# Where the rows of the stationary operand begin: a decoder block with the pads of its activation tiles taken out

## The chip, the cores and the metric

The kernel runs on one core of a Trainium2 chip. The metric is the time of one execution on the device in microseconds (us). A profile of one further execution says, engine by engine, what ran when: TensorE (PE, with its weight loads listed apart as PEld), VectorE (DVE), ScalarE (ACT), GpSimd (POOL) and SyncE (SP, which issues the transfers). A line number such as L305 is a line of the kernel's file.

## The reference

The kernel computes one decoder block for 256 tokens of width 2048, in float32:

```
mod = silu(c) @ w_ada + b_ada                      # six rows: shift, scale, gate, twice
hn  = rmsnorm(x, norm1_g) * (1 + sc1) + sh1
proj = hn @ w_in                                   # 2048 x 10256: q k v, z, beta, a, glu, two gates
o   = chunk_gated_delta_rule(...)  ;  branch_a = (norm(o) * silu(z)) @ dn_w_o
u   = causal_dwconv(val * sigmoid(gl), 31 taps) ;  branch_b = silu(layernorm(u)) @ cf_w_o
x   = x + gt1 * ((sigmoid(ga) * branch_a + sigmoid(gb) * branch_b) @ w_out)
hn  = rmsnorm(x, norm2_g) * (1 + sc2) + sh2
gate, up = split(hn @ w_up)                        # 2048 x 11264
x   = x + gt2 * ((silu(causal_dwconv(gate, 3 taps)) * up) @ w_down)      # 5632 x 2048
out = rmsnorm(x, final_norm_g)
```

## The kernel before

Nearly all of the work is products of the activations (256 tokens) with large weight matrices. `product` (L283) does each of them for 512 columns of weights at a time. It walks over the rows of the weights in chunks of two row tiles (2 x 128 rows x 512 columns). A chunk `w` is loaded by a transfer, ScalarE casts it to the rounded type fp32r (`wh`, L293), VectorE takes the difference (`wl`, L295), and TensorE then does 12 matmuls: for each row tile `kk` of the chunk and each half `t` of the tokens one of high activations with `wh` (L305), one of low activations with `wh` (L306) and one of high activations with `wl` (L307). So two rounded parts stand for each float32 number. `w`, `wh` and `wl` are rings of 5, 3 and 3 buffers in the pool `p0`.

In these matmuls the activations are the stationary operand: 128 rows (features) by 128 columns (tokens) are loaded into the array, and 512 columns of weights stream through as the moving operand. So each matmul has a weight load, and in the trace the load for the next matmul lies beside the matmul before it.

The stationary operands are tiles with a high and a low part. `hn` holds both for all 16 row tiles, of 256 tokens each, in one tile; `mg` (the merged mixers, for `w_out`) and `hn2` (for the feed-forward part) use the same place later (tag "hn", L345, L826, L871). In the program before, this tile has a pad of one number behind each row tile: `[P, 2, KD, S + 1]`, of which 0 to S are used. The products over it are called p1, qkv, glu, gb, z, ga (all over `w_in`), out, up1, gate and up. Some of them go over the row tiles in parts (0 to 3, 4 to 9, 10 to 15, `R3`), as the modulation gets ready; others over all 16 at once.

The other stationary operands are `cfh` and `cfl` (L813, L814; product cfo with `cf_w_o`), `oh0`, `ol0`, `oh1`, `ol1` (L794 to L798; product dno with `dn_w_o`) and `h` (L933; product down with `w_down`). `h` is made for each group `g` of 512 columns of the feed-forward part, in a high and a low tile of 4 row tiles each; the last product goes over groups 0 to 5 in a first half and 6 to 10 in a second, with tiles h0 to h5 used again. ScalarE writes the high parts by a cast (L936 for `h`, L263 for `hn`), VectorE the low parts by a difference (L937, L264).

The order of the instructions on each engine is set when the program is built, by a scheduler that follows priorities (the `Band` objects) and its own estimate of times. The places of the tiles in the on-chip memory follow from the pools: each tag has a place of the size of its largest tile, in the order in which the tags first appear. So `hn`'s size decides where the rings `w`, `wh` and `wl` behind it begin.

In the program before, `hn` begins at byte 40160 of each partition, the buffers of `wh` at 97632, 101728 and 105824, those of `wl` at 109920, 114016 and 118112. All of these are 96 past a multiple of 128. The tiles `h`, `oh`, `ol`, `cfh` and `cfl` all begin 64 past a multiple of 128.

Of the kernel before, what the change touches and what calls it, by code (L numbers as in the profile page):

```python
# [9 lines left out]
F32R = mybir.dt.float32r  # L10
# [4 lines left out]
P = 128  # L15
D = 2048
S = 256
KD = D // P
# [4 lines left out]
FF = 5632  # L23
FT = FF // P
EPS = 1e-6
C_Z, C_B, C_GLU, C_GA, C_GB = 3072, 4096, 4112, 6160, 8208

VEC = {}
# [27 lines left out]
def block_kernel(ctx: ExitStack, tc, x, vec, ab, rowv, w_ada, w_in, dn_w_o, cf_w_o, w_out, w_up, w_down, out):  # L56
# [6 lines left out]
    p0 = ctx.enter_context(tc.tile_pool(name="p0", bufs=1))  # L63
# [43 lines left out]
    eps = p0.tile([P, 1], F32, name="eps")  # L107
    nc.gpsimd.memset(eps, EPS)
    mone = p0.tile([P, 16], F32, name="mone")
# [115 lines left out]
    def rstd_col(ss):  # L225

        a = p0.tile([P, 2], F32, tag="nrm_a", name="nrm_a")
        nc.vector.tensor_reduce(out=a, in_=ss, axis=mybir.AxisListType.X, op=ALU.add)
        nc.gpsimd.tensor_scalar(out=a, in0=a, scalar1=1.0 / D, scalar2=EPS, op0=ALU.mult, op1=ALU.add)
        r = p0.tile([P, 2], F32, tag="nrm_c", bufs=3, name="nrm_c")  # L230
# [3 lines left out]
    def rstd_of(pt, pool=pd, tag="dl"):  # L234

        a = p0.tile([P, 2], F32, tag="nrm_a", name="nrm_a")
        nc.vector.tensor_scalar(out=a, in0=pt[:, 0:2], scalar1=EPS, scalar2=None, op0=ALU.add)
        return spread(a, pool, tag)
# [80 lines left out]
    p1 = mix.enter_context(tc.tile_pool(name="p1", bufs=1))  # L319
    su = tc.tile_pool(name="su", bufs=1)  # L320
    sup = su.__enter__()
    with b_first():
        x_sb = p0.tile([P, KD, S], F32, tag="x", name="x_sb")
        xv = x.rearrange("(t p) n -> p t n", p=P)
        xt = p1.tile([P, 2, D], F32, tag="HS", name="xt")
        for q in range(2):
            for t in range(2):
                nc.sync.dma_start(out=xt[:, t, q * 1024:(q + 1) * 1024], in_=xv[:, t, q * 1024:(q + 1) * 1024])
        nc.sync.dma_start(out=vt, in_=vec)
        ss1 = p0.tile([P, 2, 2], F32, name="ss1")  # L330
        for q in range(2):
            for t in range(2):
                sq = p1.tile([P, 1024], F32, tag=("QA", "KA")[t], name="sq")
                nc.scalar.activation(out=sq, in_=xt[:, t, q * 1024:(q + 1) * 1024], func=AF.Square, accum_out=ss1[:, t, q:q + 1])
        r1 = rstd_col(ss1)
        for q in range(4):
            qs = slice(q * 512, (q + 1) * 512)
            for t in range(2):
                nc.vector.tensor_scalar(out=xt[:, t, qs], in0=xt[:, t, qs], scalar1=r1[:, t:t + 1], scalar2=None, op0=ALU.mult)
            for i in range(2):  # L340
                k = 4 * q + 2 * i
                nc.scalar.copy(out=x_sb[:, k:k + 2, :], in_=turned(xt, (k, k + 1), pd, f"dl{i}"))
        for j in (1, 0):
            drain(ada_block(j, 0, sup, 6, shared=True))
        hn = p0.tile([P, 2, KD, S + 1], F32R, tag="hn", name="hn")[:, :, :, 0:S]  # L345
        modulate(0)
    hh, hl = (lambda k: hn[:, 0, k, :]), (lambda k: hn[:, 1, k, :])

# [14 lines left out]
    def into(parts, add):  # L363

        def evac(pts):
            for d, pt in zip(parts, pts):
                if add:
                    with b_first():
                        nc.vector.tensor_tensor(out=d, in0=pt, in1=d, op=ALU.add)
                else:  # L370
                    nc.scalar.copy(out=d, in_=pt)
        return evac

    def both(t, g=0):
        return [t[:, i, 512 * g:512 * (g + 1)] for i in range(2)]
# [415 lines left out]
        product("z", rows(w_in, C_Z + 512 * g), whole, hh, hl, evac)  # L791
        zs.append(z)
    with b_delta():
        oh0 = p1.tile([P, 4, S], F32R, tag="VA", name="oh0")  # L794
        ol0 = p1.tile([P, 4, S], F32R, tag="QB", name="ol0")
        delta_out(0, on0, zs[0], oh0, ol0)
        oh1 = p1.tile([P, 4, S], F32R, tag="QA", name="oh1")
        ol1 = p1.tile([P, 4, S], F32R, tag="KA", name="ol1")  # L798
        delta_out(1, on1, zs[1], oh1, ol1)

    half8 = (0, 8)
# [8 lines left out]
    with b_delta():  # L810
        cfs = []
        for g in range(4):
            hi = p1.tile([P, 2, S], F32R, tag=f"u{g}", name="cfh")  # L813
            lo = p1.tile([P, 2, S], F32R, tag=f"gl1{g}", name="cfl")  # L814
            nc.scalar.copy(out=hi, in_=cfa[g])
            nc.vector.tensor_tensor(out=lo, in0=cfa[g], in1=hi.bitcast(F32), op=ALU.subtract)
            cfs.append((hi, lo))
# [5 lines left out]


    side_rate[0] = 0.7
    mg = p0.tile([P, 2, KD, S + 1], F32R, tag="hn", name="mg")[:, :, :, 0:S]  # L826
    for g in range(4):
        def evac(pts, g=g):
            for pt, a, b in zip(pts, both(ga, g), both(gb, g)):
# [36 lines left out]
    p2 = ctx.enter_context(tc.tile_pool(name="p2", bufs=1))  # L866
    spare.append(True)
    gt_home[5] = lambda piece: p2.tile([P, 512], F32, tag=f"gt{piece}", name="gt2")
    with b_first():
        r2 = rstd_col(ss2)  # L870
    hn2 = p0.tile([P, 2, KD, S + 1], F32R, tag="hn", name="hn2")[:, :, :, 0:S]  # L871

    def modulate2(part):
        k0, k1 = R3[part]
# [23 lines left out]
    for half, (g0, g1) in enumerate(((0, 6), (6, 11))):  # L898
        nt = 4 * (g1 - g0)
        hf = {}  # L900
        for g in range(g0, g1):
            sg = p2.tile([P, 4, S], F32, tag="fsg", bufs=2, name="fsg")
            ks = last if g < NG else whole
            side_rate[0] = 0 if g < NG else 0.4

            def whole_sums(pts, g, i):
                if g < NG:
                    into(both(pre[2 * g + i]), True)(pts)
                    return pre[2 * g + i]
                t = p2.tile([P, 2, 512], F32, tag=f"h5{i}", name="sums")  # L910
                into(both(t), False)(pts)
                return t

            def evac_gate(pts, g=g, sg=sg):
                src = whole_sums(pts, g, 0)
                for h in range(2):
                    bank = turned(src, (2 * h, 2 * h + 1))
                    for u in range(2):
                        j = 2 * h + u
                        n = (4 * g + j) * 3  # L920
                        nc.scalar.activation(out=sg[:, j, :], in_=bank[:, u, :], func=AF.Copy, scale=V("ffconv", n + 2))
                        for sft in (1, 2):
                            nc.vector.scalar_tensor_tensor(
                                out=sg[:, j, sft:], in0=bank[:, u, 0:S - sft], scalar=V("ffconv", n + 2 - sft), in1=sg[:, j, sft:], op0=ALU.mult, op1=ALU.add)
                nc.scalar.activation(out=sg, in_=sg, func=AF.Silu)

            def evac_up(pts, g=g, sg=sg):
                src = whole_sums(pts, g, 1)
                for h in range(2):
                    bank = turned(src, (2 * h, 2 * h + 1), pd, f"dl{h}")  # L930
                    s2 = sg[:, 2 * h:2 * h + 2, :]
                    nc.vector.tensor_tensor(out=s2, in0=bank, in1=s2, op=ALU.mult)
                hf[g - g0] = [p2.tile([P, 4, S], F32R, tag=f"h{g - g0}{i}", name=f"h{g}{i}") for i in range(2)]  # L933
                for i in range(2):
                    sl = slice(2 * i, 2 * i + 2)
                    nc.scalar.copy(out=hf[g - g0][0][:, sl, :], in_=sg[:, sl, :])  # L936
                    nc.vector.tensor_tensor(out=hf[g - g0][1][:, sl, :], in0=sg[:, sl, :], in1=hf[g - g0][0][:, sl, :].bitcast(F32), op=ALU.subtract)  # L937

            product("gate", rows(w_up, 512 * g), ks, gh, gl, evac_gate)
            product("up", rows(w_up, FF + 512 * g), ks, gh, gl, evac_up)  # L940
        if half == 0:
            raw = p2.tile([P, 2, D], F32, tag="raw", name="raw")
            for g in range(4):
                product("down", rows(w_down, 512 * g, 4 * g0), (0, nt), lambda k: hf[k // 4][0][:, k % 4, :], lambda k: hf[k // 4][1][:, k % 4, :], into(both(raw, g), False))
            continue
        need((5, 0), (5, 1))
        fg_row = p2.tile([P, D], F32, name="fg_row")
        nc.sync.dma_start(out=fg_row, in_=rowv[:, 2 * D:].to_broadcast([P, D]))
        with b_ada():
            for g in range(4):  # L950
                for d, r in zip(both(raw, g), both(res, g)):
                    nc.vector.tensor_tensor(out=d, in0=d, in1=gt_row(5, g), op=ALU.mult)
                    nc.vector.tensor_tensor(out=r, in0=d, in1=r, op=ALU.add)
        for g in range(4):
            def evac(pts, g=g):
                add_to_res(5, g, ss3)(pts)
                with b_first():
                    for r in both(res, g):
                        nc.vector.tensor_tensor(out=r, in0=r, in1=fg_row[:, 512 * g:512 * (g + 1)], op=ALU.mult)
            product("down", rows(w_down, 512 * g, 4 * g0), (0, nt), lambda k: hf[k // 4][0][:, k % 4, :], lambda k: hf[k // 4][1][:, k % 4, :], evac)  # L960
# [53 lines left out]
```

## Time and profile before

| what | value |
|---|---|
| time, median of 3 runs (lowest, highest) | 1603.07 us (1601.51, 1603.42) |
| the profiled execution: its time, its span | 1604.07 us, 1602.4 us |
| TensorE busy | 1547.4 us, 97% of the span |
| VectorE, ScalarE busy | 1189.7 us (74%), 809.8 us (51%) |
| mean share of the TensorE clock granted | 0.991 |
| transfers | 366.59 MB, 229 GB/s |

Busy time is the time in which at least one instruction of the engine ran. Matmuls overlap in the pipeline, so the time of one matmul (some 0.4 us in the lists) is longer than the distance from its start to the next one's start; that distance is what the engine's time is made of.

### The profile page before, as it was taken

To read this page: it belongs to the slowest core of one execution; us is meant where nothing else is said; L and a number is where in the kernel's file an instruction comes from. 1 tells how busy PE (TensorE), PEld (TensorE's weight loads), DVE (VectorE), ACT (ScalarE), POOL (GpSimd) and SP (SyncE) were. 2 spreads that over 40 slices of the span, in tenths; PEclk is the share of its full clock that TensorE was granted. 3 is DMA by queue.
4 is the path that set the end of the run, shared out by engine and by line. 5 is a ranking of instruction groups with operands and counts; after the bars stand their busy time and mean duration, and the time that the engine had idled before them with its cause. 6 is when DMAs were issued, how large, how long until landed. Compare 5 with 4: busy or idle time off the path is not lost.

```text
span 1602.4 us, 20092 instructions
## 1 busy us (share of the span) xinstructions
PE 1547.4 (97%) x7198; PEld 1256.9 (78%) x7198; DVE 1189.7 (74%) x1556; ACT 809.8 (51%) x1221; POOL 56.5 (4%) x116
## 2 busy tenths in 40 slices
PE   5999999999999999999979999999999999999996
PEld 5787887788888878787758877888888788788885
DVE  5889967689998967896778789887445587755554
ACT  3554434777687555544346434555444444454442
POOL 2000000400002000000000000000000000000000
PEclk9999999999999989999989999999999999999998
DMA  9999865534467728789778899655556677555552
GB/s 335 385 346 342 267 193 176 158 113 131 148 215 228 245 92 275 259 264 320 260 261 303 299 320 305 204 162 179 185 185 228 224 256 268 191 177 186 183 189 94
DMA packets 182860, 366.59 MB, mean 229 GB/s; under 512 B 12516, under 2 KB 30948, under 8 KB 182632
## 3 DMA queue, kind: packets, MB, share of 16 engines
q1 hardware_dynamic: 182760, 365.31, 68.5%
q8 instruction: 56, 0.92, 0.2%
q14 instruction: 44, 0.36, 0.1%
HBM read 363.17 MB, written 2.10 MB: 228 GB/s over the span
## 4 chain that ended last, share of the span: by engine, by line
PE 85%; DMA 5%; DVE 5%; issue 1%; ACT 1%; POOL 1%; SPq 0%; POOLq 0%; ACTq 0%; DVEq 0%
PE mm_up L307 6%; PE mm_up L305 6%; PE mm_up L306 6%; PE mm_down L306 5%; PE mm_down L305 5%; PE mm_down L307 5%; DMA ada_w<-in_w_ada 4%; PE mm_p L307 4%; PE mm_p L305 4%; PE mm_p L306 4%; PE mm_gate L307 3%; PE mm_gate L306 3%; PE mm_gate L305 3%; PE turned L86 2%; PE mm_ga L307 2%; DVE ada_acc L166 2%
## 5 line engine op out<-in xcount | busy, mean ns | idle before, releaser
L293 ACT CAST wh<-w 128x1024 fp32r<-128x1024 f32 x488 | 512.2, 1051 | 573.9 <-PE mm_up L306 132.9
L295 DVE TENSOR_TENSOR wl<-w,wh 128x1024 fp32r<-128x1024 f32 x488 | 594.2, 1222 | 254.7 <-ACT wh L293 251.8
L166 DVE SCALAR_TENSOR_TENSOR ada_acc<-ada_w,c_act,ada_acc 128x768 f32<-128x768 f32 (+2 forms) x236 | 243.0, 1030 | 84.5 <-DMA ada_w<-in_w_ada 81.3
L305 PE MATMUL mm_up<-wh,hn 128*128 128x512 f32 x472 | 187.8, 400 | 0.4 <-ACT hn L263 0.4
L306 PE MATMUL mm_up<-wh,hn 128*128 128x512 f32 x472 | 187.6, 397 | 0.0
L307 PE MATMUL mm_up<-wl,hn 128*128 128x512 f32 x472 | 174.9, 399 | 0.4 <-DVE wl L295 0.4
L305 PE MATMUL mm_down<-wh,h 128*128 128x512 f32 x352 | 139.8, 397 | 0.0
L306 PE MATMUL mm_down<-wh,h 128*128 128x512 f32 x352 | 139.5, 396 | 0.0
L307 PE MATMUL mm_down<-wl,h 128*128 128x512 f32 x352 | 126.3, 397 | 0.0
L305 PE MATMUL mm_p<-wh,hn 128*128 128x512 f32 x280 | 111.7, 402 | 2.1 <-ACT hn L263 2.0
L306 PE MATMUL mm_p<-wh,hn 128*128 128x512 f32 x280 | 111.1, 399 | 0.0
L305 PEld LDWEIGHTS mm_up<-wh,hn 128*128 128x128 f32 x472 | 89.2, 189 | 21.5 <-ACT hn L263 0.8
L307 PEld LDWEIGHTS mm_up<-wl,hn 128*128 128x128 f32 x472 | 88.7, 188 | 22.1 <-DVE wl L295 1.6
L306 PEld LDWEIGHTS mm_up<-wh,hn 128*128 128x128 f32 x472 | 88.8, 188 | 20.9 <-issue 0.5
L307 PE MATMUL mm_p<-wl,hn 128*128 128x512 f32 x280 | 100.8, 401 | 0.6 <-DVE wl L295 0.5
L305 PE MATMUL mm_gate<-wh,hn 128*128 128x512 f32 x232 | 92.2, 397 | 0.0
L306 PE MATMUL mm_gate<-wh,hn 128*128 128x512 f32 x232 | 91.7, 395 | 0.0
L307 PE MATMUL mm_gate<-wl,hn 128*128 128x512 f32 x232 | 86.0, 397 | 0.0
L307 PEld LDWEIGHTS mm_down<-wl,h 128*128 128x128 f32 x352 | 66.3, 188 | 16.1
L306 PEld LDWEIGHTS mm_down<-wh,h 128*128 128x128 f32 x352 | 66.3, 188 | 16.0
L305 PEld LDWEIGHTS mm_down<-wh,h 128*128 128x128 f32 x352 | 66.3, 188 | 16.0
L428 DVE SCALAR_TENSOR_TENSOR cfa<-u,vt,cfa 128x256 f32<-128x256 f32 x176 | 76.2, 481 | 0.3
(309 smaller groups left out, 2491.8 us busy)
## 6 DMA issues: line engine op xcount, KB each, us to landing
w<-in_w_up SPq DMA_DIRECT2D x176, 512.0 KB, 4.6
w<-in_w_in SPq DMA_DIRECT2D x130, 512.0 KB, 4.3
ada_w<-in_w_ada SPq DMA_DIRECT2D x96, 512.0 KB, 5.0
ada_w<-in_w_ada SPq DMA_DIRECT2D x128, 384.0 KB, 5.3
w<-in_w_down SPq DMA_DIRECT2D x88, 512.0 KB, 3.6
w<-in_w_in SPq DMA_DIRECT2D x64, 256.0 KB, 3.7
w<-in_w_out SPq DMA_DIRECT2D x32, 512.0 KB, 5.7
w<-in_cf_w_o SPq DMA_DIRECT2D x16, 512.0 KB, 4.3
```

What stands on the lines that cost most here:

```text
L86: nc.tensor.transpose(out=out, in_=in_, identity=ident[0:n, 0:n])
L166: nc.vector.scalar_tensor_tensor(out=acc[:, 0:n], in0=wt[:, i, :], scalar=c_act[:, k:k + 1], in1=acc[:, 0:n], op0=ALU.mult, op1=ALU.add)
L293: nc.scalar.copy(out=wh, in_=w)
L295: nc.vector.tensor_tensor(out=wl, in0=w, in1=wh.bitcast(F32), op=ALU.subtract)
L305: nc.tensor.matmul(pts[t], lhsT=xh(k)[:, ts], rhs=wh[:, kk, :], start=(k == k0), stop=False)
L306: nc.tensor.matmul(pts[t], lhsT=xl(k)[:, ts], rhs=wh[:, kk, :], start=False, stop=False)
L307: nc.tensor.matmul(pts[t], lhsT=xh(k)[:, ts], rhs=wl[:, kk, :], start=False, stop=(k == k1 - 1))
L428: nc.vector.scalar_tensor_tensor(out=acc[:, i, :], in0=us[g][:, i, k:k + S], scalar=V("cfconv", (2 * g + i) * CFK + k), in1=acc[:, i, :], ...
```

## The change

Three kinds of edit, all of them on where a tile's rows begin.

First, `hn`, `mg` and `hn2` lose the pad: the row tiles are 256 numbers apart instead of 257. The tile gets 128 bytes smaller, and everything behind it in the pool moves by 128 bytes; `wh` and `wl` then begin at 97504 and 109792 (again 96 past a multiple of 128).

Second, a helper `at` makes a tile that is `room` numbers larger than it needs to be and returns the part that begins `first` numbers into it.

Third, `h`, `oh`, `ol`, `cfh` and `cfl` are made by it. The table `H_AT` has the starts of h0 to h5, `CF_AT` those of `cfh`, `O_AT` those of `oh0`, `ol0`, `oh1`, `ol1`.

```
+H_AT, CF_AT, O_AT = (9, 10, 11, 12, 14, 4), (0, 16, 32, 48), (0, 8, 8, 0)
...
-        hn = p0.tile([P, 2, KD, S + 1], F32R, tag="hn", name="hn")[:, :, :, 0:S]
+        hn = p0.tile([P, 2, KD, S], F32R, tag="hn", name="hn")
...
+    def at(pool, n, first, room, tag, name):
+
+        t = pool.tile([P, n * S + room], F32R, tag=tag, name=name)
+        return t[:, first:first + n * S].rearrange("p (n s) -> p n s", n=n)
...
-        oh0 = p1.tile([P, 4, S], F32R, tag="VA", name="oh0")
-        ol0 = p1.tile([P, 4, S], F32R, tag="QB", name="ol0")
+        oh0 = at(p1, 4, O_AT[0], 8, "VA", "oh0")
+        ol0 = at(p1, 4, O_AT[1], 8, "QB", "ol0")
...
-        oh1 = p1.tile([P, 4, S], F32R, tag="QA", name="oh1")
-        ol1 = p1.tile([P, 4, S], F32R, tag="KA", name="ol1")
+        oh1 = at(p1, 4, O_AT[2], 8, "QA", "oh1")
+        ol1 = at(p1, 4, O_AT[3], 8, "KA", "ol1")
...
-            hi = p1.tile([P, 2, S], F32R, tag=f"u{g}", name="cfh")
-            lo = p1.tile([P, 2, S], F32R, tag=f"gl1{g}", name="cfl")
+            hi = at(p1, 2, CF_AT[g], 48, f"u{g}", "cfh")
+            lo = at(p1, 2, 0, 0, f"gl1{g}", "cfl")
...
-    mg = p0.tile([P, 2, KD, S + 1], F32R, tag="hn", name="mg")[:, :, :, 0:S]
+    mg = p0.tile([P, 2, KD, S], F32R, tag="hn", name="mg")
...
-    hn2 = p0.tile([P, 2, KD, S + 1], F32R, tag="hn", name="hn2")[:, :, :, 0:S]
+    hn2 = p0.tile([P, 2, KD, S], F32R, tag="hn", name="hn2")
...
-                hf[g - g0] = [p2.tile([P, 4, S], F32R, tag=f"h{g - g0}{i}", name=f"h{g}{i}") for i in range(2)]
+                hf[g - g0] = [at(p2, 4, H_AT[g - g0], 16, f"h{g - g0}{i}", f"h{g}{i}") for i in range(2)]
```

The two built programs have the same instructions in the same order on every engine. What differs is addresses. Take the distance of an operand to be where it begins, less where the moving operand in `wh` or `wl` begins, as a remainder of 128 bytes:

| stationary operand | distance before | distance after |
|---|---|---|
| hn, mg, hn2, row tile k, high | 4k (0 to 60) | 0 |
| the same, low | 64 + 4k (64 to 124) | 0 |
| h0 to h5, high | 96 | 4, 8, 12, 16, 24, 112 |
| h0 to h5, low | 96 | 68, 72, 76, 80, 88, 48 |
| cfh of groups 0 to 3; cfl | 96; 96 | 64, 0, 64, 0; 64 |
| oh0 and ol0; oh1 and ol1 | 96; 96 | 64; 0 |

## Rows read from the trace of the kernel before

**Rows 1.** The page: its head, the engines' busy time, the chain by engine.
```profile
span 1602.4 us, 20092 instructions
...
PE 1547.4 (97%) x7198; PEld 1256.9 (78%) x7198; DVE 1189.7 (74%) x1556; ACT 809.8 (51%) x1221; POOL 56.5 (4%) x116
...
PE 85%; DMA 5%; DVE 5%; issue 1%; ACT 1%; POOL 1%; SPq 0%; POOLq 0%; ACTq 0%; DVEq 0%
```

**Rows 2.** Groups: engine, out<-in, count | busy us, mean ns | idle before.
```profile
L293 ACT CAST wh<-w 128x1024 fp32r<-128x1024 f32 x488 | 512.2, 1051 | 573.9 <-PE mm_up L306 132.9 <-PE mm_down L306 130.8 <-PE mm_p L306 63.4
...
L305 PE MATMUL mm_down<-wh,h 128*128 128x512 f32 x352 | 139.8, 397 | 0.0
...
L305 PE MATMUL mm_dno<-wh,oh 128*128 128x512 f32 x64 | 25.6, 402 | 0.0
...
L305 PE MATMUL mm_cfo<-wh,cfh 128*128 128x512 f32 x64 | 25.2, 401 | 0.9 <-ACT cfh L815 0.9
```

**Rows 3.** Timeline, one product: start us, duration us; row tiles 0 to 9, 12, end.
```profile
1240.17 0.40 PE L305 MATMUL mm_gate<-wh,hn 128*128 128x512 f32 x1
...
1241.58 0.40 PE L305 MATMUL mm_gate<-wh,hn 128*128 128x512 f32 x1
...
1242.98 0.40 PE L305 MATMUL mm_gate<-wh,hn 128*128 128x512 f32 x1
...
1244.38 0.40 PE L305 MATMUL mm_gate<-wh,hn 128*128 128x512 f32 x1
...
1245.76 0.39 PE L305 MATMUL mm_gate<-wh,hn 128*128 128x512 f32 x1
...
1247.15 0.40 PE L305 MATMUL mm_gate<-wh,hn 128*128 128x512 f32 x1
...
1248.55 0.39 PE L305 MATMUL mm_gate<-wh,hn 128*128 128x512 f32 x1
...
1249.94 0.39 PE L305 MATMUL mm_gate<-wh,hn 128*128 128x512 f32 x1
...
1251.40 0.39 PE L305 MATMUL mm_gate<-wh,hn 128*128 128x512 f32 x1
...
1252.80 0.39 PE L305 MATMUL mm_gate<-wh,hn 128*128 128x512 f32 x1
...
1256.97 0.39 PE L305 MATMUL mm_gate<-wh,hn 128*128 128x512 f32 x1
...
1258.35 0.40 PE L305 MATMUL mm_gate<-wh,hn 128*128 128x512 f32 x1
...
1262.53 0.39 PE L305 MATMUL mm_up<-wh,hn 128*128 128x512 f32 x1
```

**Rows 4.** Timeline of TensorE in the first mm_down: two starts, 14 steps apart.
```profile
1187.23 0.39 PE L305 MATMUL mm_down<-wh,h 128*128 128x512 f32 x1
...
1190.51 0.39 PE L307 MATMUL mm_down<-wl,h 128*128 128x512 f32 x1
```

**Rows 5.** Timeline of TensorE, three passes of row 0: first, cheapest, last.
```profile
60.55 0.40 PE L305 MATMUL mm_p<-wh,hn 128*128 128x512 f32 x1
...
61.95 0.40 PE L305 MATMUL mm_p<-wh,hn 128*128 128x512 f32 x1
...
1287.46 0.39 PE L305 MATMUL mm_gate<-wh,hn 128*128 128x512 f32 x1
...
1288.83 0.39 PE L305 MATMUL mm_gate<-wh,hn 128*128 128x512 f32 x1
...
1451.70 0.39 PE L305 MATMUL mm_up<-wh,hn 128*128 128x512 f32 x1
...
1453.09 0.40 PE L305 MATMUL mm_up<-wh,hn 128*128 128x512 f32 x1
```

**Rows 6.** ScalarE's casts by tile: count, ns least/median/most, first and last start.
```profile
L263 ACT CAST hn<-t x32: 390/407/429, 40.5 to 976.9; 128x256 fp32r<-128x256 f32 x32
...
L936 ACT CAST h<-fsg x22: 612/621/625, 1020.6 to 1482.6; 128x512 fp32r<-128x512 f32 x22
```

## The prediction

> **What bounds the kernel now.** I read the page first. The span is 1602.4 us, TensorE is busy for 1547.4 us of it (97%), and the chain of waits runs through TensorE for 85% of the span [rows 1]. So time is won or lost where TensorE spends its steps, not in a wait. Next, the groups of instructions: 488 casts of a chunk of weights [rows 2], each of which feeds 12 matmuls of 128x512, make 5856 of them. mm_down is 3 x 352 = 1056, mm_dno and mm_cfo are 3 x 64 each, 384 together [rows 2]; that leaves 4416 for the products whose stationary operand is a row of hn or mg. TensorE stands idle for 0.0 us before the matmuls of mm_down and mm_dno shown and 0.9 us before those of mm_cfo [rows 2], so inside these products next to nothing is waited for.
>
> Then the timeline of one product that nothing interrupts, 96 matmuls from 1240.17 to 1262.53 us [rows 3]. What counts is the step, the time from one matmul's start to the next one's: 22.36 us / 96 = 232.9 ns. The duration beside each (0.39, 0.40) overlaps the next and is not the step. The loading of the stationary operands, 1256.9 us for 7198 of them [rows 1] or 175 ns each, lies beside the matmuls. Each row k of hn serves six matmuls in a row (three for each half of the tokens), and the starts listed are those of a row's first matmul. Row 7 needs 1.46 us for its six, 243.3 ns a step; row 12 needs 1.38 us, 230.0 ns; the others lie between, from 1.38 to 1.41 us (a listed start is good to 0.01 us, 1.7 ns a step). The work of a row is the same for every row; what differs is where it starts. In the program before, rows are 257 numbers apart, and the rings wh and wl begin at 96 bytes past a multiple of 128, so the high part of row k begins 4k bytes past the rings' remainder (of 128 bytes), and its low part 4k + 64. In mm_down every operand, high and low, stands at 96. There 14 steps take 1190.51 - 1187.23 = 3.28 us [rows 4], 234.3 ns each. So the step depends on the distance by a few ns, and a few ns on 5856 steps are what this change is about: 1 ns on all is 5.9 us, 0.37%.
>
> **The change, part by part.** No instruction is added, taken away or moved: the order on every engine is the same, and the queues too. What moves is addresses.
>
> Rows of hn, mg and hn2 without pads. All 16 rows, high and low, now stand at distance 0, where only the high part of row 0 stood. The trace shows row 0 in 29 undisturbed passes, the first 1.40 us for six (60.55 to 61.95), the last 1.39 us, the cheapest 1.37 us (1287.46 to 1288.83) [rows 5], the dearest 1.41 us [rows 3]; their mean is 232.6 ns a step. That is my value: 4416 x (232.6 - 232.9) = -1.3 us. It contains the loss of row 7's excess (10.4 ns in one row of 16, 0.65 ns in the mean, 2.9 us) and the loss of the cheap rows beside it. What the trace does not show is a low part at distance 0, and 4416 steps without a change of distance. From below, the cheapest row there is: all at 230.0 gives -12.8 us. From above, the dearest: all at row 7's 243.3 gives +46 us. None of row 0's passes comes near that; the dearest, 1.41 us, would be 235.0 ns and +9 us. I stay with row 0's mean, the nearest row, and keep 228.3 (the 1.37 us pass) to 235.0 for the range.
>
> The operands of mm_down. Groups g = 0 to 5 of each half go from distance 96 to 4, 8, 12, 16, 24 and 112 bytes, the low parts 64 further on (the last one 64 back, at 48). The first five are what rows 1, 2, 3, 4 and 6 of hn have now, high and low alike; the last is row 12 with the two exchanged. In the product of [rows 3] these rows need 1.40, 1.40, 1.38, 1.39, 1.39 and 1.38 us. The first half has all six groups, the second half the first five: (2 x (233.3 + 233.3 + 230.0 + 231.7 + 231.7) + 230.0) / 11 = 231.8 ns, against 234.3. 1056 x -2.5 = -2.6 us. From both sides: 230.0 gives -4.5 us, 235.0 gives +0.7 us.
>
> The operands of mm_cfo and mm_dno go from 96 to 0 or 64. No row has high and low both at these; by row 0 again 384 x (232.6 - 234.3) = -0.7 us; between -1.7 us (at 230.0) and +0.3 us (at 235.0).
>
> What writes these tiles. ScalarE's casts into hn take 390 to 429 ns at 16 different starts [rows 6], and those into h are 612 to 625 ns [rows 6]; in hn the start leaves no trace, so the new starts of h (36, 40, 44, 48, 56, 16 bytes into the tile) cost nothing that I can see. Were they slower, the products of gate and up lie beside them, and mm_down reads its first group long after it was written; only the last group's casts stand near mm_down's start, and even these are read last of all. The larger tiles of h, oh, ol and cfh take room, not time.
>
> Sum: -1.3 - 2.6 - 0.7 = -4.6 us on the profiled execution, which took 1604.07 us (1.7 us of it outside the span); 1599.5 us. That execution is 1.0 us above the median of the runs, 1603.07, so against the median I predict 1598.5 us. Every us counts in full, since TensorE is in the chain almost everywhere; the 15% where it isn't would take back at most 0.7 us.
>
> **The rivals.**
> A. The start has no effect, and rows 7 and 12 differ for another reason. Then the time stays at 1603 us. For it: the change touches no work. Against it: row 7 is slow with the same instructions as its neighbours, which are not [rows 3]. The Trainium skill has this rule (SBUF — State Buffer, "Who interferes with whom"): TensorE reads its moving operand and its stationary operand through two independent ports and never waits on anyone. By that rule no distance could matter; the 243.3 ns beside 230.0 ns speak against it.
> B. One distance for all locks the steps into a pattern that is dearer than the mixture. mm_down has that now: high and low at one distance, and 234.3 ns, where row 8 of hn, whose low part alone stands at that 96, needs 1.40 us, 233.3 ns [rows 3, 4]: the pattern itself seems to cost about 1 ns. If hn does as mm_down does, 4416 x 1.4 = +6.2 us; with -2.6 us from mm_down and 0 for the other two, +3.6 us: 1606.7 us. At row 0's dearest pass, 235.0 ns in hn and in mm_cfo and mm_dno, it is 1610 us (+9.3 - 2.6 + 0.3). It decides from a mean step of 234.3 ns in hn's products on: there the loss eats the gain and 0.2% more.
> C. One distance locks them into a cheaper pattern, as the pass of 1.37 us had it for a moment [rows 5]. At 231 ns: 4416 x -1.9 = -8.4 us, with the other terms 1591 us; at 228.3 ns, 1580 us.
>
> **How the numbers follow.** What a measurement here can tell from no change is about 0.2%, 3.2 us. The forecast gets 0.44; its own range is 1595 to 1603 us, of which 0.27 lies over 0.2% faster and 0.17 within. A gets 0.08, within. B gets 0.29: 0.27 slower, 0.02 within. C gets 0.19, faster. So faster 0.46, same 0.27, slower 0.27. The range of 8 in 10 reaches into B and C: from 1588 us (hn near 230.3 ns, the other terms as forecast) to 1610 us (hn at 235.0 ns).
>
> **What would show it right or wrong.** In the timeline of a product over hn, row 7's long steps are gone, and every row's six matmuls take the same time, 1.39 to 1.40 us; the product's 96 steps take 22.3 us. In mm_down the steps differ by group, below 234.3 ns on average. Casts into h stay at 621 ns, the idle time of TensorE as it is. The prediction is wrong if hn's products run at 234.3 ns or more, if they fall to 231 ns, or if row 7 still stands out.

## The result, and the profile after

The changed kernel takes 1584.4 us (median of 4 runs, 1582.0 to 1589.8) against 1602.4 us for the kernel before on the same chip: a ratio of 0.9892, with an interval of 0.9866 to 0.9919. I had forecast 1598.5 us with a range from 1588 to 1610. The sign was right; the gain was 18 us where I had 4.6, and the range missed it.

The head of the page, the engines' busy time and the chain by engine, of the kernel after, to be held against [rows 1]:

```profile
span 1582.4 us, 20092 instructions
...
PE 1520.4 (96%) x7198; PEld 1250.5 (79%) x7198; DVE 1187.3 (75%) x1556; ACT 809.1 (51%) x1221; POOL 57.1 (4%) x116
...
PE 75%; DMA 9%; DVE 9%; issue 3%; ACT 2%; POOL 1%; SPq 0%; DVEq 0%; POOLq 0%; ACTq 0%
```

The same number of instructions. Of the busy times TensorE's falls most, from 1547.4 to 1520.4 us, 27.0 less; that of its loads falls by 6.4, VectorE's by 2.4. The span falls by 20.0 only. So two things want explaining: why the steps became so much shorter, and where 7 us of it went. The second shows in the chain already: TensorE has 75% of it instead of 85%, and DMA and VectorE have 9% each instead of 5%.

The timeline of the product that answers to [rows 3], in the kernel after; start and duration in us, then line, operation and tiles. The starts are those of the first of a row's six matmuls, of rows 0, 1, 2, 6, 7, 8, 12 and 13, and of the next product:

```profile
1226.54 0.40 PE L307 MATMUL mm_gate<-wh,hn 128*128 128x512 f32 x1
...
1227.92 0.39 PE L307 MATMUL mm_gate<-wh,hn 128*128 128x512 f32 x1
...
1229.28 0.39 PE L307 MATMUL mm_gate<-wh,hn 128*128 128x512 f32 x1
...
1234.72 0.39 PE L307 MATMUL mm_gate<-wh,hn 128*128 128x512 f32 x1
...
1236.08 0.39 PE L307 MATMUL mm_gate<-wh,hn 128*128 128x512 f32 x1
...
1237.44 0.39 PE L307 MATMUL mm_gate<-wh,hn 128*128 128x512 f32 x1
...
1242.88 0.39 PE L307 MATMUL mm_gate<-wh,hn 128*128 128x512 f32 x1
...
1244.24 0.39 PE L307 MATMUL mm_gate<-wh,hn 128*128 128x512 f32 x1
...
1248.32 0.39 PE L307 MATMUL mm_up<-wh,hn 128*128 128x512 f32 x1
```

Each row now takes 1.36 us for its six, 226.7 ns a step; only row 0 takes 1.38, with the first steps after mm_down in it. Row 7 is no longer to be told from its neighbours. The 96 steps take 21.78 us, 226.9 ns each, where they took 22.36. There is no wait in this product before or after; the steps themselves are shorter. Nor is it the clock: in this product, and from the end of mm_up's second pass up to it, the granted clock is 1.00 in both kernels. In these rows, of that stretch before and after, it is the third number from the end:

```profile
991.60:1240.20 248.60, 248.60 (x1118) 201.41 (x1117) 159.52 (x190) 115.98 (x135) 0.00 (x0) 1.00 0.60 196
```

```profile
981.60:1226.50 244.90, 244.90 (x1117) 201.02 (x1116) 159.62 (x191) 115.94 (x134) 0.00 (x0) 1.00 0.61 200
```

Below, "the step" of a product is the mean time from one matmul's start to the next one's, over all neighbours in the trace with nothing between them and less than 300 ns apart. Over the whole program it falls from 233.15 to 227.78 ns in the products with hn, mg and hn2, from 234.27 to 231.23 in mm_down, and from 234.1 to about 231.6 in mm_cfo and mm_dno. By the counts of the prediction that is 4416 x -5.37 = -23.7 us, 1056 x -3.04 = -3.2 us and 384 x -2.5 = -1.0 us: -27.9 us together.

### The profile page after: what moved, and what is told of

Its sections match the earlier page's. It is cut to its first block, busy times and chain, and to the rows that moved or that the text cites. A ratio compares the mean times of both kernels' runs of the same rounds, so it can differ in the third digit from the quotient of the medians.

```text
span 1582.4 us, 20092 instructions
## 1 busy us (share of the span) xinstructions
PE 1520.4 (96%) x7198; PEld 1250.5 (79%) x7198; DVE 1187.3 (75%) x1556; ACT 809.1 (51%) x1221; POOL 57.1 (4%) x116
## 4 chain that ended last, share of the span: by engine, by line
PE 75%; DMA 9%; DVE 9%; issue 3%; ACT 2%; POOL 1%; SPq 0%; DVEq 0%; POOLq 0%; ACTq 0%
DMA ada_w<-in_w_ada 8%; PE mm_down L309 5%; PE mm_down L308 5%; PE mm_down L307 5%; PE mm_up L307 5%; PE mm_up L309 5%; PE mm_up L308 5%; PE mm_p L309 3%; PE mm_gate L307 3%; PE mm_gate L309 3%; PE mm_gate L308 3%; PE mm_p L307 3%; PE mm_p L308 3%; DVE ada_acc L168 3%; DVE wl L297 3%
## 5 line engine op out<-in xcount | busy, mean ns | idle before, releaser
L297 DVE TENSOR_TENSOR wl<-w,wh 128x1024 fp32r<-128x1024 f32 x488 | 592.7, 1220 | 238.7 <-ACT wh L295 232.1
L168 DVE SCALAR_TENSOR_TENSOR ada_acc<-ada_w,c_act,ada_acc 128x768 f32<-128x768 f32 (+2 forms) x236 | 242.5, 1028 | 90.8 <-DMA ada_w<-in_w_ada 88.4
L307 PE MATMUL mm_up<-wh,hn 128*128 128x512 f32 x472 | 186.0, 396 | 0.4 <-ACT hn L265 0.4
L308 PE MATMUL mm_up<-wh,hn 128*128 128x512 f32 x472 | 185.6, 393 | 0.0
L307 PE MATMUL mm_p<-wh,hn 128*128 128x512 f32 x280 | 109.7, 395 | 2.1 <-ACT hn L265 2.0
L308 PE MATMUL mm_p<-wh,hn 128*128 128x512 f32 x280 | 109.1, 391 | 0.0
L308 PEld LDWEIGHTS mm_up<-wh,hn 128*128 128x128 f32 x472 | 89.0, 188 | 18.5 <-issue 0.5
```

The lines of the kernel that those rows point to most:

```text
L168: nc.vector.scalar_tensor_tensor(out=acc[:, 0:n], in0=wt[:, i, :], scalar=c_act[:, k:k + 1], in1=acc[:, 0:n], op0=ALU.mult, op1=ALU.add)
L297: nc.vector.tensor_tensor(out=wl, in0=w, in1=wh.bitcast(F32), op=ALU.subtract)
L307: nc.tensor.matmul(pts[t], lhsT=xh(k)[:, ts], rhs=wh[:, kk, :], start=(k == k0), stop=False)
L308: nc.tensor.matmul(pts[t], lhsT=xl(k)[:, ts], rhs=wh[:, kk, :], start=False, stop=False)
```

## The experiments

Three theories went in. Theory 1: the step is set by the distance from the start of the moving operand (in the rings) to the start of the stationary one, and one particular distance gives a short step. Against it stood that it is the even spacing of the rows, that it is the place in memory itself, and that the other tiles earned the gain. Theory 3: the 7 us are lost between mm_cfo and mm_up, where transfers set the pace. ("Theory 2" was the even spacing; it is the rival of the third run.)

This table has what the runs that settle the first question gave. "Place" is the distance just described, high part / low part, modulo 256 bytes; why 256 is what the runs below show. The ratio is to the kernel before, with its interval.

| kernel | place of hn, mg, hn2 | their step, ns | place of h | mm_down's step, ns | median us | ratio |
|---|---|---|---|---|---|---|
| before | 128+4k / 192+4k | 233.15 | 96 / 96 | 234.3 | 1602.4 | |
| after | 0 / 0 | 227.8 | six different | 231.2 | 1584.4 | 0.9892 [0.9866, 0.9919] |
| pads out | 0 / 0 | 227.85 | 96 / 96 | 234.3 | 1588.0 | 0.9908 [0.9890, 0.9927] |
| others moved | 128+4k / 192+4k | 233.1 | six different | 231.3 | 1600.4 | 0.9986 [0.9973, 0.9999] |
| hn at 96 | 224 / 224 | 233.3 | 96 / 96 | 234.2 | 1603.8 | 1.0005 [0.9993, 1.0017] |
| row 0 everywhere | 128 / 192 | 232.95 | 96 / 96 | 234.3 | 1602.8 | 1.0004 [0.9992, 1.0015] |
| both moved | 0 / 0 | 227.8 | 96 / 96 | 234.3 | 1588.3 (one run) | |
| one spacer | 0 / 0 | 227.8 | 0 / 0 | 226.8 | 1577.6 | 0.9844 [0.9831, 0.9857] |

**Which part of the change.** The first run makes one half of it, the second the other.

```diff
-        hn = p0.tile([P, 2, KD, S + 1], F32R, tag="hn", name="hn")[:, :, :, 0:S]
+        hn = p0.tile([P, 2, KD, S], F32R, tag="hn", name="hn")
...
```

> The kernel before with only the pads of hn, mg and hn2 taken out; every other tile starts where it did. Theory 1 (the lock): the step of a product with hn, mg or hn2 is set by the distance, modulo 128 bytes, from the moving ring's start to the stationary start; with that distance at 0 for every row the step falls from 233.2 to about 226.7 ns, as in the changed kernel. 4,416 steps then give about -27 us of TensorE's busy time; mm_down, whose distance stays 96, stays at 234.3 ns. Of the whole about 8 us are lost again between mm_cfo and mm_up as in the changed kernel, so 1586 to 1589 us. Rival (the prediction's own sum): the row tiles are worth only -1.3 us and the gain came from the other tiles: 1600 to 1602 us.

Measured: 1588.0 us; hn's step 227.85 ns, mm_down's 234.3. The prediction's own sum falls; what it is about the row tiles that counts, this run doesn't tell. One product over hn in it, from its first start to the next product's, is 21.79 us, 227.0 ns a step:

```profile
1228.85 0.39 PE L305 MATMUL mm_gate<-wh,hn 128*128 128x512 f32 x1
...
1250.64 0.39 PE L305 MATMUL mm_up<-wh,hn 128*128 128x512 f32 x1
```

The second run is the changed kernel with the pads put back in hn, mg and hn2, and oh and ol at their old starts:

```diff
-        hn = p0.tile([P, 2, KD, S], F32R, tag="hn", name="hn")
+        hn = p0.tile([P, 2, KD, S + 1], F32R, tag="hn", name="hn")[:, :, :, 0:S]
...
```

> The changed kernel with the pads of hn, mg and hn2 put back, and with oh and ol at their old starts: only the h tiles (mm_down) and cfh, cfl (mm_cfo) begin elsewhere. Theory 1: hn's products stay at 233.2 ns, mm_down falls from 234.3 to 231.2 ns over 1,056 steps (-3.3 us) and mm_cfo by about 2 ns over 192 (-0.4 us): 1598 to 1600 us, little or nothing of the change's -18 us. Rival (the gain came from the other tiles): 1585 to 1588 us.

Measured: 1600.4 us, hn's step 233.1 ns, mm_down's 231.3, mm_cfo's 232.6. The two halves, -14 and about -2 us, make up nearly all of the change's -18: the row tiles without pads are what counts.

**Spacing or distance.** The tile of the first run gets 128 bytes of room, and its rows, still 256 numbers apart, begin 24 numbers later:

```diff
+    HN_HI, HN_LO = 24, 24
...
+        n = KD * S
+        t = p0.tile([P, 2 * n + 32], F32R, tag="hn", name=name)
+        return [t[:, i * n + a:(i + 1) * n + a].rearrange("p (k s) -> p k s", k=KD) for i, a in enumerate((HN_HI, HN_LO))]
...
```

> The kernel before without pads, as in the first of these runs, but all of hn, mg and hn2 begin 24 numbers (96 bytes) later: rows are still 256 numbers apart, and the distance to the rings is 96 for every row in place of 0. Theory 1 (distance): hn's step becomes what mm_down showed at 96, 231 to 238 ns in turn, mean 234.3, against 233.2 before: 4,416 x 1.1 = +5 us, 1605 to 1609 us. Rival (it is the even spacing of the rows, 256 instead of 257 numbers, not where they begin): step 226.7 to 228 ns, 1585 to 1589 us.

Measured: 1603.8 us, no change from before, and hn's step is 233.3 ns. The spacing is the same as in the first run and all its gain is gone: it is where the rows begin. (The room moves the rings as well, so the place is 224 modulo 256, and 96 only modulo 128; that this matters I learned from the next runs.) A product in this run takes 22.40 us, 233.3 ns a step:

```profile
1239.91 0.39 PE L313 MATMUL mm_gate<-wh,hn 128*128 128x512 f32 x1
...
1262.31 0.40 PE L313 MATMUL mm_up<-wh,hn 128*128 128x512 f32 x1
```

**Which distance.** Each of the six h buffers serves one or two groups of 96 steps of mm_down, so one run can try six distances. In the first such run the high and the low part have starts of their own, and each tile 128 bytes of room:

```diff
-H_AT, CF_AT, O_AT = (9, 10, 11, 12, 14, 4), (0, 16, 32, 48), (0, 8, 8, 0)
+H_AT, CF_AT, O_AT = ((8, 8), (16, 16), (24, 24), (12, 12), (20, 20), (28, 28)), (0, 16, 32, 48), (0, 8, 8, 0)
...
```

> The changed kernel with the high and the low part of each h tile at one and the same distance from the rings: 0, 32, 64, 16, 48 and 80 bytes (modulo 128) for the six buffers in turn, each of which serves one or two groups of 96 steps of mm_down. Theory 1: the group at 0 runs at 226.7 ns as hn does; a constant distance always locks into one short cycle, so every group has a step of its own, between 226.7 and about 240 ns, the same in both of its groups to 0.3 ns. Rival (mm_down is slower for another reason, the three-slot rings or the tile's four blocks, and the start has no part in it): all groups within 1 ns of each other at 231 to 234 ns. The whole run at 1579 to 1590 us by either.

Measured: 1587.4 us in one run. The group "at 0" ran at 232.8 and 233.6 ns, not 226.7, and its two groups differ by more than the 0.3 ns that I had allowed; the others at 233.2, 231.6, 231.6, 230.4 and 231.4. Theory 1 as I had put it fell, and so did its rival, since the groups differ by 3 ns. Looking again at the addresses, the high and the low part of each group stood 128 bytes apart modulo 256: the same remainder of 128, but not the same place. And hn at 0 modulo 128 was at 0 modulo 256, 512 and 1024 as well. So the next run set the distances modulo 512, by a lead ahead of each high part (32, 64, 64, 128, 128, 64 bytes, which add up from tile to tile):

```diff
-H_AT, CF_AT, O_AT = (9, 10, 11, 12, 14, 4), (0, 16, 32, 48), (0, 8, 8, 0)
+H_AT, CF_AT, O_AT = ((8, 0), (16, 0), (16, 0), (32, 0), (32, 0), (16, 0)), (0, 16, 32, 48), (0, 8, 8, 0)
...
```

> The changed kernel with the high and the low part of each h tile at the same distance from the rings modulo 512 bytes: 128, 192, 256, 384, 0 and 64 for the six buffers in turn. The first sweep set distances modulo 128 only. Theory 1 refined: the groups at 0 run at 226.7 ns like hn at 0, and the groups at 128, 192, 256, 384 and 64 at other, higher steps, 229 to 235 ns. Rival (mm_down cannot come under 229 ns, because of its own rings or evictions): the group at 0 is at 229 to 234 ns like its neighbours. The whole run at 1578 to 1590 us.

The timeline of one product of mm_down in that run; these are the first matmuls of six groups of 24 steps, at 128, 192, 256, 384, 0 and 64, and of what follows:

```profile
1123.45 0.39 PE L307 MATMUL mm_down<-wh,h 128*128 128x512 f32 x1
...
1129.02 0.39 PE L307 MATMUL mm_down<-wh,h 128*128 128x512 f32 x1
...
1134.53 0.39 PE L307 MATMUL mm_down<-wh,h 128*128 128x512 f32 x1
...
1139.99 0.40 PE L307 MATMUL mm_down<-wh,h 128*128 128x512 f32 x1
...
1145.58 0.39 PE L307 MATMUL mm_down<-wh,h 128*128 128x512 f32 x1
...
1151.03 0.40 PE L307 MATMUL mm_down<-wh,h 128*128 128x512 f32 x1
...
1156.63 0.39 PE L307 MATMUL mm_down<-wh,h 128*128 128x512 f32 x1
```

The run took 1581.6 us, once. The groups take 5.57, 5.51, 5.46, 5.59, 5.45 and 5.60 us: per step 232.1, 229.6, 227.5, 232.9, 227.1 and 233.3 ns. The cheap ones are 256 and 0, and 384 is like 128: the period is 256 bytes. Over all 96 steps of each the means are 227.1 and 227.3 ns at 0, 227.5 at 256. mm_down comes down as far as hn does, and the rival falls.

The third such run looks beside the good place:

> The changed kernel with high and low parts of the h tiles at the same distance modulo 256: 156, 224, 240, 4, 16 and 32 for the six buffers in turn. Theory 1 with modulus 256: 224 gives 233.3 ns, as hn gave at 480; 156, where row 7 stood before, is the dearest of the six, 235 ns or more; 4 lies within 2 ns of the 227.3 at 0. Rival (modulus 512, or only the exact distance 0 and 256 is cheap): 224 away from 233.3 by over 1 ns, 4 at 230 ns or more.

Measured: 1585.1 us in one run. 224 gives 233.2 and 233.5 ns in its two groups, as hn gave in the third run: a period of 256 again. But 4 bytes off the good place is 232.4 ns already, in both groups; there I was wrong and the rival's 230 ns or more was right: it is a narrow place upwards. Sixteen bytes below it, at 240, the groups have 227.6 and 229.3; at 16, 233.2 and 234.0; at 32, 233.3. And 156, the place of row 7's high part before (its low part stood at 220), has two answers in one program; I had expected it to be the dearest. Its two groups of mm_down, 24 steps from the first start to the second in each half:

```profile
1126.44 0.39 PE L307 MATMUL mm_down<-wh,h 128*128 128x512 f32 x1
...
1131.89 0.39 PE L307 MATMUL mm_down<-wh,h 128*128 128x512 f32 x1
...
1484.85 0.43 PE L307 MATMUL mm_down<-wh,h 128*128 128x512 f32 x1
...
1490.67 0.40 PE L307 MATMUL mm_down<-wh,h 128*128 128x512 f32 x1
```

That is 227.1 ns a step in one and 242.5 in the other, with the same tiles, instructions and distances. So a distance does not always fix the step. Nor is it the tile's own place: in the first product of the second half the same tile ran its first 17 steps at 226.6 ns in the mean, then TensorE did a turn (a transpose) between two of them. That costs two long steps in either half; behind them the steps were 255, 266, 244 and 230 ns here, and 235 and 231 in the first half. What came ahead may decide between the two patterns; no run tests that.

**The prediction's own place for all rows.** The kernel of "hn at 96" with other starts: without pads, the high part of every row where that of row 0 stood, and the low part 64 bytes further:

```diff
-    HN_HI, HN_LO = 24, 24
+    HN_HI, HN_LO = 0, 16
```

> The kernel before without pads, with every row of hn, mg and hn2 where its row 0 stood before: the low part 64 bytes further on than the high part, modulo 128, and the distances to the rings 384 and 448 modulo 512. This is the place that the prediction priced when it took row 0's mean of 232.6 ns for all rows. Theory 1 as refined after the first sweep (the step depends on the distance modulo 512, and 0 is the good one): hn's step 230 to 233.3 ns as in row 0's three passes before, 1590 to 1602 us. Theory 1 as first put (modulo 128, a constant distance locks): about 226.7 to 228 ns, 1584 to 1589 us.

Measured: 1602.8 us, as before the change. A product in that run, from its first start to the next product's:

```profile
1237.64 0.40 PE L313 MATMUL mm_gate<-wh,hn 128*128 128x512 f32 x1
...
1260.04 0.39 PE L313 MATMUL mm_up<-wh,hn 128*128 128x512 f32 x1
```

22.40 us for 96 steps, 233.3 ns; over the program 232.95. That is what I had priced (232.6), and it is not the place to which the change moves the rows.

**Distance or place in memory.** The tile of hn gets a lead of 24 numbers and no other room, so that hn, the rings and all that lies behind them move together by 96 bytes, modulo 256.

```diff
+        t = p0.tile([P, 2 * KD * S + 24], F32R, tag="hn", name=name)
+        return t[:, 24:].rearrange("p (i k s) -> p i k s", i=2, k=KD)
...
-        hn = p0.tile([P, 2, KD, S + 1], F32R, tag="hn", name="hn")[:, :, :, 0:S]
+        hn = rows_at("hn")
...
```

> The kernel before without pads, with hn, mg, hn2 and the rings all 96 bytes further on (modulo 256), so that their distance is still 0. Theory 1 (distance between the two reads): hn's step stays at 227 to 228 ns, mm_down at 234.3, the whole at 1584 to 1590 us. Rival (the place itself, modulo 256, of one of the two decides): hn's step leaves 227 ns by more than 2 ns, and with over 230 ns the whole is at 1595 us or more.

Measured: 1588.3 us in one run, hn's step 227.8 ns, mm_down's 234.3: as in the first run. For this one shift it is the distance, not the place. The second row of a product in it takes 1.36 us for its six matmuls, 226.7 ns a step:

```profile
1228.69 0.39 PE L310 MATMUL mm_gate<-wh,hn 128*128 128x512 f32 x1
...
1230.05 0.39 PE L310 MATMUL mm_gate<-wh,hn 128*128 128x512 f32 x1
```

**Where 7 us went.** The product stages from mm_cfo to the second pass of mm_up are 1,476 steps. By their means these are 7.2 us shorter after than before, yet the stretch takes as long. By engine in that stretch: the columns are the stretch, its length, busy us of TensorE, of its loads, of VectorE, ScalarE and GpSimd (with counts), the granted clock, the share of the DMA engines and GB/s. The kernel before, and then the one after:

```profile
599.20:991.60 392.40, 375.29 (x1688) 298.18 (x1689) 321.46 (x386) 182.00 (x267) 5.79 (x10) 0.99 0.84 284
```

```profile
588.60:981.60 393.00, 372.25 (x1689) 297.89 (x1690) 320.25 (x385) 181.75 (x268) 6.50 (x9) 0.98 0.84 283
```

The transfers ran at 284 and 283 GB/s, their engines busy for 0.84 of the time in both. The waits in these stretches, with us in total, times and the longest, before and after:

```profile
DVE ada_acc L166 <- DMA ada_w<-in_w_ada: 56.8, 46, 3.8
...
PE mm_out L307 <- DVE wl L295: 3.3, 4, 1.4
...
PE mm_cfo L307 <- DVE wl L295: 0.9, 2, 0.5
...
PE mm_up L307 <- DVE wl L295: 0.4, 1, 0.4
```

```profile
DVE ada_acc L168 <- DMA ada_w<-in_w_ada: 60.8, 47, 4.0
...
PE mm_out L309 <- DVE wl L297: 4.5, 6, 1.8
...
PE mm_up L309 <- DVE wl L297: 2.5, 6, 1.1
...
PE mm_cfo L309 <- DVE wl L297: 1.9, 2, 1.4
```

TensorE waits more often for the low part of the weights, which VectorE makes, and VectorE itself waits longer for the side stream's tiles, ada_w. (The side stream is w_ada, from which the modulation is made: it is fetched in pieces beside the products, and VectorE adds up its products with silu(c).) Gaps of 300 ns or more between two neighbouring matmuls of a product add up, beyond a step of 230 ns each, to 11.2 us before and 18.5 us after in this stretch: 7.3 us more, nearly the whole of the loss. It is no accident of one trace: the four kernels of this document with the long step in hn have 11.2 to 12.7 us of such gaps there, and the seven with the short step and the same stream 16.7 to 21.1. To see whether the transfers are behind it, half of the side stream's were left out in both kernels, after its first two blocks. Each piece that arrives is used twice, so that the sums are not the reference's:

```diff
-                wt = pool.tile([P, step, n], F32, tag="ada_w", bufs=bufs, name="ada_w")
-                last_ada[0] = nc.sync.dma_start(out=wt, in_=av[:, kc:kc + step, c0:c0 + n]).ins
+                if shared or kc // step % 2 == 0:
+                    wt = pool.tile([P, step, n], F32, tag="ada_w", bufs=bufs, name="ada_w")
+                    last_ada[0] = nc.sync.dma_start(out=wt, in_=av[:, kc:kc + step, c0:c0 + n]).ins
```

> The kernel before with half of the transfers of the w_ada side stream left out after the first two blocks: each tile that arrives is used for two steps, so VectorE's work and its order stay and the sums are not the reference's. Theory 3 (between mm_cfo and mm_up the transfers bound the changed kernel, so its shorter steps bought nothing there): the kernel before gains little, 1590 to 1602 us, and the changed kernel with the same cut gains 5 to 9 us more than it does. Rival (VectorE's splits and sums bound that stretch): neither gains more than 2 us beyond the other.

> The changed kernel with the same half of the side stream's transfers left out. Theory 3: the difference to the kernel before with the same cut grows from 18 to 23 to 27 us, and the stages from mm_cfo to the second pass of mm_up, which gained nothing, are now 6 to 9 us shorter than in that kernel; 1567 to 1577 us. Rival (VectorE bounds that stretch): the difference stays at 16 to 20 us and the stages stay as long.

Measured: 1597.5 us for the kernel before (0.9966 [0.9956, 0.9976]) and 1573.7 us for the changed one (0.9822 [0.9807, 0.9836]), both ratios to the kernel before with the whole stream: a difference of 23.9 us instead of 18.0. The stretch in the two, as above:

```profile
596.40:980.90 384.50, 373.04 (x1684) 299.78 (x1685) 326.29 (x390) 182.27 (x265) 6.91 (x10) 0.98 0.70 233
```

```profile
590.30:971.40 381.10, 367.89 (x1685) 300.08 (x1686) 325.03 (x390) 182.23 (x266) 6.68 (x9) 0.98 0.71 235
```

With VectorE's work as it was, the stretch is now 3.4 us shorter after than before, where it had been 0.6 longer, and VectorE's waits for ada_w fall to 18.9 and 22.5 us. The gaps are 4.9 and 8.4 us: the loss there is 3.5 instead of 7.3. By these two traces the transfers account for about half of it, where Theory 3 expected the stretch to be 6 to 9 us shorter. By the medians the difference of the two kernels grows by 5.9 us, to 23.9, which lies in Theory 3's range (23 to 27 us) and out of the rival's (16 to 20). The traces don't bear that growth out: the profiled execution of the kernel before with half the stream, 1593.4 us, is the fastest of its ten, 4.1 us below their median: the two profiled spans, 1591.7 and 1572.0 us, are 19.7 us apart, no more than the 20.0 with the whole stream. So the transfers have a part in the loss; how large it is, one trace of each kernel doesn't settle, and what holds back the rest was not told apart.

**A version that beats both.** If 0 modulo 256 is the good place, one tile of 160 bytes that nothing uses, laid behind the rings, brings every stationary tile of the program there. This is the first run with:

```diff
+    space = p0.tile([P, 40], F32, name="space")
+    nc.gpsimd.memset(space, 0.0)
     last, whole = R3[2], (0, KD)
```

> The kernel before without pads, and one unused tile of 160 bytes behind the rings, which brings every stationary tile of every product (hn, mg, hn2, h, oh, ol, cfh, cfl) to a distance of 0 modulo 256. Theory 1: mm_down, mm_dno and mm_cfo fall from 234.2 to 227.3 ns too; 1,056 x 7 = -7.4 us of mm_down count in full against the run with the pads out (1588.0), and of the 384 x 7 = -2.7 us of the other two nearly nothing, since they lie where the transfers take it back (Theory 3): 1578 to 1583 us, under the changed kernel's 1584.4. Rival (those tiles gain only what the changed kernel's starts gave them): 1584 to 1588 us.

Measured: 1577.6 us, 0.9844 of before; its interval and that of the changed kernel do not touch. The head and the engines of its page, and 24 steps of mm_down, which are 5.44 us or 226.7 ns each where they are 5.62 in the first run:

```profile
span 1574.9 us, 20093 instructions
...
PE 1514.0 (96%) x7198; PEld 1250.9 (79%) x7198; DVE 1187.8 (75%) x1556; ACT 809.3 (51%) x1221; POOL 56.7 (4%) x117
```

```profile
1123.35 0.39 PE L305 MATMUL mm_down<-wh,h 128*128 128x512 f32 x1
...
1128.79 0.39 PE L305 MATMUL mm_down<-wh,h 128*128 128x512 f32 x1
```

mm_down is at 226.8 ns over all its steps, mm_cfo and mm_dno at 228.1. The median is 10.5 us below the first run's; mm_down explains 1056 x 7.5 = 7.9 us, and the other 2.6 are about what the 384 steps of mm_cfo and mm_dno gained. I had expected these to be lost again, and they were not.

The last run gives that kernel another pace of the side stream, to fetch earlier what the busy stretch lacks:

```diff
-    side[0], side_rate[0] = ada_blocks([(2, 0), (2, 1), (4, 0), (3, 0), (4, 1), (3, 1), (4, 2), (3, 2), (5, 0), (5, 1)], p0, 2, b_ada), 0.6
+    side[0], side_rate[0] = ada_blocks([(2, 0), (2, 1), (4, 0), (3, 0), (4, 1), (3, 1), (4, 2), (3, 2), (5, 0), (5, 1)], p0, 2, b_ada), 0.85
...
-        side_rate[0] = (1.3,0.9)[part]
+        side_rate[0] = (1.1,0.85)[part]
```

> The kernel with the one spacer, and the side stream's pace changed: 0.85 in place of 0.6 steps per pair of weight rows during mm_ga, then 1.1 and 0.85 in place of 1.3 and 0.9 in the two passes of mm_up that add up rows 0 to 9. Theory 3 (the stretch from mm_cfo to mm_up is bound by transfers, and mm_ga has room): some of the 7 us lost there come back, 1573 to 1579 us. Rival (mm_ga's own waits grow by as much, or VectorE bounds the stretch): 1579 to 1586 us, no faster than with the spacer alone.

Measured: 1593.1 us, 0.9938 [0.9921, 0.9954], 15.5 us worse than with the spacer alone and beyond what either side expected. One wait of TensorE, in the stretch from 680 to 820 us, is most of it:

```profile
PE pt L86 <- DVE ada_acc L166: 13.6, 1, 13.6
```

With the stream further on, the turns (transposes) of the second of its blocks that are turned stand earlier in mm_out, behind 48 of its 384 matmuls in place of 145 with the spacer alone. TensorE, which has them in its order there, waits for VectorE's sums and these for the stream. The pace decides where such turns stand in TensorE's order, not only when transfers start. This run is therefore no test of Theory 3.

## Why the prediction was wrong

Point by point, as it put them.

- "The step depends on the distance by a few ns": right, and this is all that the change is about. No order changed, and the casts into h took 622 ns in the median after, 621 before [rows 6].
- "All 16 rows, high and low, now stand at distance 0 ... row 0 ... their mean is 232.6 ns a step. That is my value": this is the step that failed. I measured distance by the remainder of 128 bytes. The runs show a period of 256, and by that row 0 stood at 128 and 192, and the change moves the rows to 0 and 0, where no row of any operand had stood. With all rows at row 0's old place the step is 232.95 ns, so the number was good for its place; the place was another one. Nor would a low part at 0 have been enough: in the first sweep of mm_down the group with its high part at 128 and its low part at 0 ran at 233 ns. The term was to be -1.3 us and measures -23.7.
- "From below, the cheapest row there is: all at 230.0": the bound came from the same rows and was none. The step at the new place, 226.7 ns, lies under every row mean that I used. Only the pass of 1.37 us (228.3 ns) [rows 5] pointed that way, and I gave what it pointed to, rival C, a chance of 0.19. Rival C is what happened: one distance for all locks the steps into a cheaper pattern. That its 228.3 ns comes so near to the 227.8 measured is luck: the pass stood at 128 and 192, where a whole kernel runs at 232.95. Its price at 228.3 ns, 1580 us, came out low against 1584.4 because of the loss in the point on "every us" below.
- "The operands of mm_down": forecast 231.8 ns and -2.6 us, measured 231.2 and -3.2 us. By buffer the forecasts were 233.3, 233.3, 230.0, 231.7, 231.7 and 230.0; measured 233.5 (the mean of its two groups), 231.1, 229.1, 232.4, 230.4 and 231.0. Modulo 256 the buffers 0, 2 and 4 really stand where rows 1, 3 and 6 of hn stood, and 1, 3 and 5 don't; those three are off by -2.2, 0.7 and 1.0 ns, the three that do by 0.2, -0.9 and -1.3, and the mean by only 0.6 because these errors partly cancel. The term came out near; reading prices off rows did not prove itself by it.
- "The operands of mm_cfo and mm_dno": -0.7 us forecast, about -1.0 measured.
- "Every us counts in full ... would take back at most 0.7 us": the 0.7 was 15% of the small gain forecast. The steps gave 27.9 us and the span 20.0, so 7.9 came back, where 15% of 27.9 would be 4.2: the share too was put too low. From mm_cfo to mm_up 7.3 us came back as waits, in part tied to the side stream's transfers.
- Rival A, that the start has no effect, is out. The rule of the Trainium skill that stood beside it (SBUF — State Buffer, "Who interferes with whom": two independent ports, one for the moving operand and one for the loading of the stationary one) does not hold for these runs as I read it: with the same work the step goes from 226.7 to 234.3 ns by the distance between the two starts alone. That the ports themselves are where this comes from no run shows. Rival B, a lock into a dearer pattern, did not come: at 0 the lock is cheap. mm_down at 96 has such a pattern (234.3 ns); hn at 224 ("hn at 96") runs at 233.3 ns, no dearer than the mixture's 233.15.
- The marks: row 7's long steps are gone, as said; "1.39 to 1.40 us" for a row and "22.3 us" for the product are 1.36 and 21.78. Its own condition for being wrong, a fall to 231 ns, is met.

Not shown by any run: what makes the step depend on the distance, whether one of TensorE's two reads gives way to the other, and why the period is 256 bytes. The loads take 188 ns in mm_down in every kernel.

## What to carry to other kernels

Where TensorE alternates loads and matmuls without a wait, look at the start-to-start step, not at the durations, and at where both operands begin: moving addresses alone took the step from 233 to 227 ns and 1.6% off the time (1602.6 to 1577.6 us). A price read off neighbouring rows held here only for the rows' very places, compared by the right period, so try a constant distance over a whole product before trusting a mixture. And before counting a shorter step in full, find the stretch that other work already holds to the old pace: here 7 of 28 us came back as waits.

## What was not expected of the hardware

- The step depends on the distance between the two operands' starts with a period of 256 bytes: 226.7 ns at 0 and 227.5 at 256, 232.4 at 4, 233 to 234.3 at 16, 32, 64 and 96, 232.4 at 128 and 232.9 at 384, 229.4 at 192, 233.3 at 224, 227.6 to 229.3 at 240 (mm_down's groups, high and low part at the same distance).
- The same distance can give two steady patterns: at 156 bytes 227.1 ns in one group of mm_down and 239.9 in the other (means over their 96 steps).
- Moving both operands by 96 bytes leaves the step as it was (227.8 ns in hn's products, one run).
